# Queueing the scaling of a token tile behind a convolution on VectorE, in the first half of a feed-forward layer

## The chip, the cores and the metric

The kernel runs on one core of one Trainium2 chip. The metric is the device time of one execution in microseconds (us). The core has TensorE (PE in the profile, with its weight loads as PEld), VectorE (DVE), ScalarE (ACT), GpSimd (POOL) and SyncE (SP), which issues nearly all transfers. Each engine works through its own queue in the order that the program was given when it was built.

## The reference, cut to what matters

One layer of a hybrid encoder over 2048 tokens (16 learned ones are put ahead of them) of width 1024. The change lies in its feed-forward half:

```python
f = causal_dwconv(rms_norm(h, norm_ffn_pre[l]) @ ffn_up[l], ffn_conv[l])   # 1024 -> 2 x 2816, 3 taps
gate, val = jnp.split(f, 2, axis=-1)
f = (jax.nn.gelu(gate, approximate=True) * val) @ ffn_down[l]
h = h + rms_norm(f, norm_ffn_post[l])
```

`rms_norm` divides each token by the root of its mean square and multiplies it by a learned gain.

## The kernel before, in words

**Stages.** Input projection, three mixers and the output projection (`w_out_tile`) come first; this last one leaves the hidden state in the scratch array `scr_h`. The up-projection `ffn_up` follows, and then the down-projection. In the profiled run the up-projection runs from 1682 to 2592 us.

**Units.** `ffn_up` works in three super-blocks (`sup`) of 684 tokens each, and in each on 22 column blocks (`j`). One pair (sup, j) is called a unit here, and the units are numbered 0 to 65. A unit has 7 products of 12 matmuls, 84 in all, written to `psu` in three PSUM banks. A Strassen-like scheme makes 7 products do the work of 8, in fp32 split into a high and a low part. PE's queue interleaves the products of neighbouring units. Because products share banks, VectorE and ScalarE act between them: `ga`, `vb` and `u2` are copied out by ScalarE (L1768), and VectorE adds them back (L1784, L1787, L1790). The last product of a unit, p4, goes into a bank that L1787 (written `vb<-psu,vb`) has to have read first. So PE waits there if VectorE is late.

**VectorE in a unit.** Apart from those additions it makes the low parts of the weights (`uw<-uq,uw`, L1603, behind a ScalarE copy, L1602), and two multiply-adds for each of the four convolved blocks (`uy`, L1738, behind ScalarE's L1736). The last of these eight operations reads p4's result, so it stands where p4 of the unit is done. GpSimd multiplies gate by value (L1744), does some of the splits, and makes sums of weights.

**Token tiles.** The tokens of the next super-block are got ready while the current one is computed. The function `between`, called at the head of each unit, fetches the first tile of 128 tokens at j = 1, and at each of j = 2 to 7 fetches one more and calls `ffn_norm` on the one fetched before. A fetch (`ffn_fetch`, L1557, 512 KB from `scr_h` into `xt`) goes through SP's queue. Three buffers hold `xt`. `ffn_norm` scales the tile on VectorE in place (L1564, `xt<-xt,rsv,g_fpre`: by the token's factor `rsv` and by the gain), lets PE transpose it in 8 pieces (L1569, `pst<-ident,xt`), and copies the transposed pieces into `q` (L56 on ScalarE, L58 on VectorE). Super-blocks 1 and 2 have six tiles each. The seven tiles of super-block 0 are scaled during the output projection.

**What sets the order.** A scheduler orders the queues when the program is built: it simulates the engines by its own durations, and hands an engine the next instruction that it takes to be ready. A scaling has no link to the unit in which it is written but the arrival of its tile, so it can be put far ahead of that unit. The context `tc.issue_after(ins)` adds the rule that what is written in it is queued behind `ins` on that engine; it adds no wait at run time.

Of the kernel before, what the change touches and what calls it, by code (L numbers as in the profile page):

```python
# [13 lines left out]
ALU = mybir.AluOpType  # L14
# [155 lines left out]
def mm3(nc, out, ah, al, bh, bl, first, last, more=False):  # L170

    nc.tensor.matmul(out, ah, bh, start=first, stop=False, skip_group_check=more)  # L172
    nc.tensor.matmul(out, ah, bl, start=False, stop=False, skip_group_check=more)  # L173
    nc.tensor.matmul(out, al, bh, start=False, stop=last, skip_group_check=more)  # L174
# [264 lines left out]
class Attn:  # L439
# [43 lines left out]
    def next(self, s):  # L483
        self.turn[s] = (self.turn[s] + 1) % len(self.ring[s])
        return self.ring[s][self.turn[s]]
# [1067 lines left out]
def ffn_fetch(core, pool, scr, s, rows):  # L1553

    xt = pool.tile([P, D], F32, tag="nt_x", name=core.n("xt"))
    t0 = s + META - HALO
    core.nc.sync.dma_start(xt[:rows], scr["h"][t0 : t0 + rows, :])  # L1557
    return xt


def ffn_norm(core, psum, xt, s, rows, rs, gain, quarters, sup):

    nc = core.nc
    nc.vector.scalar_tensor_tensor(xt[:rows], xt[:rows], rs[:rows], gain[:rows], op0=ALU.mult, op1=ALU.mult)  # L1564
    for half in range(2):
        ps = psum.tile([P, 4, P], F32, tag="mm", name=core.n("pst"))
        for k in range(HK):
            k0 = P * (HK * half + k)
            nc.tensor.transpose(ps[:, k, :rows], xt[:rows, k0 : k0 + P], core.ident[:rows, :rows])  # L1569
        for i, blk in enumerate("ab"):  # L1570
            b0 = FBLK * (2 * sup + i)
            a, e = max(s, b0), min(s + rows, b0 + FN)
            if a < e:
                core.evac(quarters[f"{blk}{half}"][:, :, a - b0 : e - b0], ps[:, :, a - s : e - s])
# [5 lines left out]
def ffn_quarters(core, pool, sup):  # L1580

    t = pool.tile([P, len(QUARTERS), HK, FN], F32, tag="q", name=core.n("q"))
    q = {s: t[:, i] for i, s in enumerate(QUARTERS)}
    used = SEQ + HALO - FBLK * (2 * sup + 1)
    if used < FN:
        for s in ("b0", "b1"):
            core.nc.gpsimd.memset(q[s][:, :, used:], 0.0)
    return q
# [129 lines left out]
def ffn_up(core, raws, ring, pool, banks, w_up, cw, scr, between, tokens):  # L1718

    nc = core.nc
    tt, stt = nc.vector.tensor_tensor, nc.vector.scalar_tensor_tensor
    turn = 1
    units = [(sup, j) for sup in range(SUPERS) for j in range(NFF)]
    ahead = UpWeights(core, raws, ring, w_up, scr, 0, 0)
    ws, xs, own = [], [], ahead
    for i in range(UP_FIRST):
        xs.append(tokens(0, i))
        ws.append(ahead.operand(i))  # L1730
    xs.append(tokens(0, UP_FIRST))

    def conv(src, u, j, n):
        y = pool.tile([P, FBLK], F32, tag="uy", name=core.n("uy"), bufs=UY)
        cc = u * NFF + j
        nc.scalar.activation(y[:, :n], src[:, 2 : n + 2], AF.Copy, scale=cw[:, 88 + cc : 89 + cc])  # L1736
        for i in (1, 0):
            stt(y[:, :n], src[:, i : n + i], cw[:, 44 * i + cc : 44 * i + cc + 1], y[:, :n], op0=ALU.mult, op1=ALU.add)  # L1738
        if u == 0:
            nc.scalar.activation(y[:, :n], y[:, :n], AF.Gelu_apprx_tanh)  # L1740
        return y

    def ending(g, v, j, b0, n):
        core.pooled = nc.gpsimd.tensor_tensor(v[:, :n], g[:, :n], v[:, :n], op=ALU.mult)  # L1744
        nc.sync.dma_start(scr["ff"][P * j : P * j + P, b0 : b0 + n], v[:, :n])

    for at, (sup, j) in enumerate(units):
        b0 = [FBLK * (2 * sup + i) for i in range(2)]
        n = [min(FBLK, SEQ - b) for b in b0]
        s = lambda tag: pool.tile([P, FN], F32, tag=tag, name=core.n(tag), bufs=1 if tag == "u2" else 2)[:]  # L1750
        between(sup, j)
        more = at + 1 < len(units)
        if more:
            ahead = UpWeights(core, raws, ring, w_up, scr, *units[at + 1][::-1])
        ws_next, bank = [], {}
        turn ^= 1
        for i, (name, (_, _, at_)) in enumerate(PRODUCTS.items()):
            w, x = ws[i], xs[i]
            first = at_ not in bank
            if first:  # L1760
                bank[at_] = banks[turn].tile([P, 512], F32, tag="up", name=core.n("psu"))[:, :FN]
            ps = bank[at_]
            for k in range(HK):
                mm3(nc, ps, w[:, 0, k], w[:, 1, k], x[:, 0, k], x[:, 1, k], first and k == 0, k == HK - 1, not first)
            behind = nullcontext()
            if name in ("p1", "p5", "p6"):
                t = s({"p1": "ga", "p5": "vb", "p6": "u2"}[name])
                copied = nc.scalar.activation(t, ps, AF.Copy)  # L1768
                ga, vb, u2 = (t, None, None) if name == "p1" else (ga, t, None) if name == "p5" else (ga, vb, t)
                if at == 0:  # L1770
                    behind = core.tc.issue_after(copied.ins)
            with behind:
                if at == 0 and len(ws) < 7:
                    ws.append(own.operand(len(ws)))
                if at == 0 and len(xs) < 7:
                    xs.append(tokens(0, len(xs)))
                if j == NFF - 1 and more:
                    xs[i] = tokens(sup + 1, i)
                if more:
                    ws_next.append(ahead.operand(i))  # L1780
            if name in ("p1", "p5", "p6"):
                pass
            elif name == "p3":
                tt(ps, ps, u2, op=ALU.add)  # L1784
                gb = conv(ps, 0, j, n[1])
            elif name == "p7":
                tt(vb, ps, vb, op=ALU.add)  # L1787
                vb = conv(vb, 1, j, n[1])
            elif name == "p2":
                tt(ps, ps, ga, op=ALU.add)  # L1790
                ga = conv(ps, 0, j, n[0])
                ending(gb, vb, j, b0[1], n[1])
            else:
                va = conv(ps, 1, j, n[0])
                ending(ga, va, j, b0[0], n[0])
        ws = ws_next
# [197 lines left out]
def hybrid_block_kernel(ctx: ExitStack, tc: tile.TileContext, args, out):  # L1994
    a = {s: v[0] if s != "meta_tokens" else v for s, v in args.items()}
    nc = tc.nc
    core = Core(tc, ctx)
# [9 lines left out]
    def pool(es, name, bufs, **kw):  # L2007
        return es.enter_context(tc.tile_pool(name=name, bufs=bufs, **kw))
# [4 lines left out]
    def spread(pl, vec, name):  # L2013
        t = pl.tile([P, D], F32, name=name)
        nc.sync.dma_start(t[:], vec.rearrange("(o n) -> o n", o=1).broadcast_to([P, D]))
        return t

    rsv = base.tile([P, 6 * len(FFN_TILES)], F32, name="rsv")
    cw = base.tile([P, 3 * 2 * NFF], F32, name="ffn_cols")
# [68 lines left out]
    with ExitStack() as p3:  # L2088
        ps_n = pool(p3, "ps_n", 2, space=PSUM, **early)
# [3 lines left out]
        g_fpre = spread(pool(p3, "gf", 1, **early), a["norm_ffn_pre"], "g_fpre")  # L2093
# [6 lines left out]
        rs = {}  # L2100
        with p2:
# [8 lines left out]
            quarters = {0: ffn_quarters(core, qp, 0)}  # L2110
            for i, (f, rows) in enumerate(FFN_TILES):
# [6 lines left out]
                for _ in range(NORMS if i >= LATE else 0):  # L2118
                    if todo:
                        q, f, rows = todo.pop(0)  # L2120
                        xt = ffn_fetch(core, np_, scr, f, rows)
# [15 lines left out]
        def between(sup, j):  # L2137

            for _ in range(1 + (j % 4 == 3) if sup else 0):
                next(later, None)  # L2140
            sup += 1
            if j == 1 and sup < SUPERS:
                quarters[sup] = ffn_quarters(core, qp, sup)
                todo[:] = tiles[sup]
                fetch()
            elif j == 1:
                kept = qp.tile([P, DOWN_KEPT, 2, 512], F32R, tag="q", name=core.n("qd"))
                down.extend(kept[:, i] for i in range(DOWN_KEPT))
            elif sup == SUPERS:
                if j == DOWN_FROM:  # L2150
                    raw = lambda: tmp.tile([P, 512], F32, tag="uq", name=core.n("raw"))[:]
                    ws.append(down_operands(core, raw, lambda: down.pop(0), a["ffn_down"], scr, 0))
            elif fetched:
                q, f, rows, xt = fetched.pop(0)
                fetch()
                ffn_norm(core, ps_n, xt, f, rows, rs[q], g_fpre, quarters[sup], sup)
                if not fetched:
                    sums.append(ffn_sums(core, quarters[sup], lambda: tc.issue_after(core.pooled.ins)))
            else:
                for _ in range(2):  # L2160
                    next(sums[-1], None)
# [79 lines left out]
```

## Time and profile before

| | |
|---|---|
| median of 3 runs (range) | 3065.51 us (3058.34 to 3071.79) |
| the profiled execution's own time | 3063.42 us |
| its span, from the first to the last instruction | 3061.7 us |
| around the span | 1.7 us |
| mean granted clock of PE | 0.971 |
| busy share of PE, DVE, ACT, POOL | 95%, 67%, 48%, 45% |

"Busy" is the time in which an engine had an instruction in work. The ends of matmuls are modelled, so the number of matmuls in a stretch says more about PE's speed than its busy share. In a table of stretches each engine has its busy time and in brackets the number of its instructions. In a timeline, the square brackets give the idle time of the engine just before an instruction and what ended it.

### The profile page before, as it was taken

Reading aid. Unit: us, or ns where it says so; the run is one execution under the profiler, and the core shown is the slowest. Engines: PE = TensorE matmul, PEld = TensorE weight load, DVE = VectorE, ACT = ScalarE, POOL = GpSimd, SP = SyncE. Lnnn points to the kernel's source line nnn. Section 1 sums busy time; section 2 is a strip of 40 time slices with the busy share of each in tenths; the row PEclk is TensorE's granted clock in tenths of the full one; section 3 lists DMA queues with packets and bytes.
Section 4 is the critical chain, followed back from the end, with each engine's and each line's share of the span. In section 5 each row is a group of like instructions: output and inputs, shape, how many; then the busy total and the mean of one; then the engine's idle time right before and its main releaser. Section 6 shows DMA issues by size and latency. Waiting matters only on the chain.

```text
span 3061.7 us, 52809 instructions
## 1 busy us (share of the span) xinstructions
PE 2910.2 (95%) x18694; PEld 2487.6 (81%) x18694; DVE 2057.7 (67%) x3934; ACT 1479.1 (48%) x2853; POOL 1365.7 (45%) x1599
## 2 busy tenths in 40 slices
PE   6998999999989999999999899999999999999998
PEld 6997898888876654566568899999999999787786
DVE  5268645656677785555636888888778777547766
ACT  4245332434346554454534656666566665324333
POOL 1001121122214556566843457445645544556765
PEclk8999999999989898999999999999999999999999
DMA  6776478466654347434336555566677765535454
GB/s 216 244 234 207 163 240 292 154 199 205 211 156 92 88 105 211 109 100 122 75 94 206 171 181 180 172 202 213 209 215 212 220 192 165 171 102 175 148 162 145
DMA packets 467750, 532.58 MB, mean 174 GB/s; under 512 B 85550, under 2 KB 355576, under 8 KB 465932
## 3 DMA queue, kind: packets, MB, share of 16 engines
q1 hardware_dynamic: 466716, 528.27, 56.5%
q8 instruction: 147, 2.41, 0.3%
q14 instruction: 119, 0.97, 0.1%
q0 software_dynamic: 768, 0.93, 0.1%
HBM read 369.11 MB, written 159.95 MB: 173 GB/s over the span
## 4 chain that ended last, share of the span: by engine, by line
PE 34%; DVE 5%; DMA 5%; POOL 3%; issue 3%; ACT 1%; SPq 0%; POOLq 0%; DVEq 0%; ACTq 0%
PE psu L172 8%; PE psu L173 8%; PE psu L174 8%; PE psd L172 2%; PE psd L173 2%; PE psd L174 2%; DMA u<-scr_ff 2%; DMA xt<-scr_h 1%; DVE uw L1603 1%; PE pswo L172 1%; PE pswo L174 1%; PE pswo L173 1%; DVE fo L1603 1%; DVE uy L1738 1%; POOL u L1858 1%
## 5 line engine op out<-in xcount | busy, mean ns | idle before, releaser
L172 PE MATMUL psu<-xo,uw 128*128 128x344 f32 x1848 | 590.8, 323 | 14.7 <-DVE vb L1787 6.9
L173 PE MATMUL psu<-xo,uw 128*128 128x344 f32 x1848 | 593.1, 321 | 0.0
L174 PE MATMUL psu<-xo,uw 128*128 128x344 f32 x1848 | 584.3, 320 | 1.5 <-DVE uw L1603 1.5
L172 PE MATMUL psp<-xh,wh 128*128 128x384 f32 (+2 forms) x1152 | 383.5, 333 | 4.5 <-ACT wh L166 3.0
L174 PE MATMUL psp<-xh,wl 128*128 128x384 f32 (+2 forms) x1152 | 379.5, 330 | 2.6 <-DMA wl<-scr_wk 2.5
L173 PE MATMUL psp<-xl,wh 128*128 128x384 f32 (+2 forms) x1152 | 379.3, 329 | 0.0
L1603 DVE TENSOR_TENSOR uw<-uq,uw 128x512 fp32r<-128x512 f32 x341 | 321.0, 947 | 65.1 <-ACT uw L1602 62.8
L172 PEld LDWEIGHTS psu<-xo,uw 128*128 128x128 f32 x1848 | 347.4, 189 | 19.2 <-DVE vb L1787 9.4
L174 PEld LDWEIGHTS psu<-xo,uw 128*128 128x128 f32 x1848 | 347.2, 189 | 2.4 <-DVE uw L1603 2.3
L173 PEld LDWEIGHTS psu<-xo,uw 128*128 128x128 f32 x1848 | 348.5, 189 | 0.1
L1602 ACT ACTIVATE uw<-uq 128x512 fp32r<-128x512 f32 x462 | 287.5, 627 | 107.5 <-PE psu L174 46.6
L686 ACT ACTIVATE p<-sc,bias 128x512 f32<-128x512 f32 (+4 forms) x352 | 197.0, 589 | 194.9 <-PE sc L682 162.1
L559 DVE TENSOR_REDUCE mc<-mx 128x1 f32<-128x512 f32 (+6 forms) x352 | 190.2, 564 | 114.1 <-PE mx L554 87.2
L1738 DVE SCALAR_TENSOR_TENSOR uy<-psu,ffn_cols,uy 128x342 f32<-128x342 f32 (+1 forms) x396 | 223.7, 567 | 62.3 <-ACT uy L1736 60.9
L1744 POOL TENSOR_TENSOR uy<-uy,uy 128x342 f32<-128x342 f32 (+1 forms) x132 | 140.0, 1061 | 252.7 <-DVE uy L1738 70.1
L725 POOL TENSOR_TENSOR acc<-acc,p 128x512 f32<-128x512 f32 (+3 forms) x208 | 221.7, 1068 | 53.1 <-DVE acc L725 23.9
L1603 POOL TENSOR_TENSOR uw<-uq,uw 128x512 fp32r<-128x512 f32 x121 | 177.6, 1468 | 148.0 <-ACT uw L1602 129.5
L172 PEld LDWEIGHTS psp<-xh,wh 128*128 128x128 f32 x1152 | 221.7, 192 | 11.6 <-issue 4.2
L174 PEld LDWEIGHTS psp<-xh,wl 128*128 128x128 f32 x1152 | 220.8, 192 | 12.0 <-issue 5.7
L173 PEld LDWEIGHTS psp<-xl,wh 128*128 128x128 f32 x1152 | 221.3, 192 | 7.5 <-issue 5.4
L1603 DVE TENSOR_TENSOR fo<-u,fo 128x896 fp32r<-128x896 f32 x88 | 109.0, 1240 | 118.8 <-ACT fo L1602 118.8
L1602 ACT ACTIVATE fo<-u 128x896 fp32r<-128x896 f32 x88 | 81.1, 922 | 200.9 <-POOL u L1859 103.8
(470 smaller groups left out, 6470.3 us busy)
## 6 DMA issues: line engine op xcount, KB each, us to landing
uq<-scr_us SPq DMA_DIRECT2D x220, 256.0 KB
uq<-in_ffn_up_dram SPq DMA_DIRECT2D x209, 256.0 KB
wl<-scr_wk SPq DMA_DIRECT2D x48, 512.0 KB
wh<-scr_wk SPq DMA_DIRECT2D x48, 512.0 KB
u<-scr_ff SPq DMA_DIRECT2D x88, 256.0 KB
scr_ff<-uy SPq DMA_DIRECT2D x110, 171.0 KB
raw<-in_w_in_dram SPq DMA_DIRECT2D x24, 512.0 KB
scr_wk<-wh SPq DMA_DIRECT2D x24, 512.0 KB
```

Source lines behind the costliest of these rows:

```text
L172: nc.tensor.matmul(out, ah, bh, start=first, stop=False, skip_group_check=more)
L173: nc.tensor.matmul(out, ah, bl, start=False, stop=False, skip_group_check=more)
L174: nc.tensor.matmul(out, al, bh, start=False, stop=last, skip_group_check=more)
L559: self.reduced = nc.vector.tensor_reduce(mc[:rows, i, ci : ci + 1], ps[:rows, : e - a], axis=AX.X, op=ALU.max)
L686: last = nc.scalar.activation(p[:rows, :w], ps[:rows, :w], AF.Exp, bias=bias[:rows, j : j + 1])
L725: eng.tensor_tensor(a, ps_[0][0][:rows, c0:n] if start and i == 1 else a, p[:rows, : n - c0], op=ALU.add)
L1602: core.nc.scalar.activation(hi, src, AF.Copy)
L1603: (eng or core.nc.vector).tensor_tensor(lo, src, hi, op=ALU.subtract)
L1738: stt(y[:, :n], src[:, i : n + i], cw[:, 44 * i + cc : 44 * i + cc + 1], y[:, :n], op0=ALU.mult, op1=ALU.add)
L1744: core.pooled = nc.gpsimd.tensor_tensor(v[:, :n], g[:, :n], v[:, :n], op=ALU.mult)
L1858: tt(s3, a0, b0, op=ALU.subtract)
```

## The change

The scaling inside `ffn_norm` is put into a context given by the caller. The caller in `between` gives one that queues the scaling behind the last convolution operation traced so far, which is that of the unit ahead (unit j-1 for the tile of unit j). The calls during the output projection are left as they were. `conv` keeps the instruction in `core.conved`. No operation is added or taken away.

```diff
-def ffn_norm(core, psum, xt, s, rows, rs, gain, quarters, sup):
+def ffn_norm(core, psum, xt, s, rows, rs, gain, quarters, sup, after=nullcontext):
     nc = core.nc
-    nc.vector.scalar_tensor_tensor(xt[:rows], xt[:rows], rs[:rows], gain[:rows], op0=ALU.mult, op1=ALU.mult)
+    with after():
+        nc.vector.scalar_tensor_tensor(xt[:rows], xt[:rows], rs[:rows], gain[:rows], op0=ALU.mult, op1=ALU.mult)
...
         for i in (1, 0):
-            stt(y[:, :n], src[:, i : n + i], cw[:, 44 * i + cc : 44 * i + cc + 1], y[:, :n], op0=ALU.mult, op1=ALU.add)
+            core.conved = stt(
+                y[:, :n], src[:, i : n + i], cw[:, 44 * i + cc : 44 * i + cc + 1], y[:, :n], op0=ALU.mult, op1=ALU.add
+            )
...
-                ffn_norm(core, ps_n, xt, f, rows, rs[q], g_fpre, quarters[sup], sup)
+                behind = lambda: tc.issue_after(core.conved.ins)
+                ffn_norm(core, ps_n, xt, f, rows, rs[q], g_fpre, quarters[sup], sup, behind)
```

All line numbers of the changed kernel are higher by 1 in `ffn_norm` and by 3 behind `conv`. The scheduler makes a new order of all queues from it. Three places show how.

VectorE before, around the scaling of the fifth tile of super-block 1 (`xt_18889`, which belongs to unit 6). `uy_18542<-psu_18395` is the last convolution of unit 2; `psu_18589`, `ga_18584` and the like belong to unit 3.

```order
L1603 TENSOR_TENSOR uw_18627<-uq_18624,uw_18627 128x512
L1564 SCALAR_TENSOR_TENSOR xt_18889<-xt_18889,rsv,g_fpre 128x1024
L1738 SCALAR_TENSOR_TENSOR uy_18542<-psu_18395,ffn_cols,uy_18542 128x342
L1603 TENSOR_TENSOR uw_18645<-uq_18642,uw_18645 128x512
L1738 SCALAR_TENSOR_TENSOR uy_18542<-psu_18395,ffn_cols,uy_18542 128x342
L1603 TENSOR_TENSOR uw_18668<-uq_18565,uw_18668 128x512
L1603 TENSOR_TENSOR uw_18689<-uq_18569,uw_18689 128x512
L1790 TENSOR_TENSOR psu_18676<-psu_18676,ga_18584 128x344
L1784 TENSOR_TENSOR psu_18589<-psu_18589,u_3257_18622 128x344
```

VectorE now, around the same tile. `uy_19058<-psu_18914` is the last convolution of unit 5; `psu_19099`, `vb_19112` and the like belong to unit 6.

```order
L1604 TENSOR_TENSOR uw_19175<-uq_19173,uw_19175 128x512
L1739 SCALAR_TENSOR_TENSOR uy_19058<-psu_18914,ffn_cols,uy_19058 128x342
L1565 SCALAR_TENSOR_TENSOR xt_18889<-xt_18889,rsv,g_fpre 128x1024
L1604 TENSOR_TENSOR uw_19198<-uq_19196,uw_19198 128x512
L1787 TENSOR_TENSOR psu_19099<-psu_19099,u_3335_19131 128x344
L1793 TENSOR_TENSOR psu_19183<-psu_19183,ga_19092 128x344
L1604 TENSOR_TENSOR uw_19268<-uq_19245,uw_19268 128x512
L1739 SCALAR_TENSOR_TENSOR uy_19156<-psu_19099,ffn_cols,uy_19156 128x342 x2
L58 COPY q_18219<-pst_19073 128x4x128
L1790 TENSOR_TENSOR vb_19112<-psu_19079,vb_19112 128x344
```

The scaling stood ahead of the last convolution of unit 2, four units before its own; it stands behind that of unit 5 now. All twelve go the same way. In super-block 1 each of the six is now queued at the head of its own unit, 2 to 7. Before, its first three were queued during the output projection, the fourth in unit 0 and the fifth and sixth in units 3 and 4, and the first three tiles of super-block 2 in units 5, 6 and 7, sixteen units and more ahead of theirs. All six of super-block 2 are now queued in units 24 to 29.

PE before, at the transposes of the first tile of super-block 1 (`xt_18220`): in unit 0, between its second and third product.

```order
L173 MATMUL psu_18069<-xo_18019,uw_18025 128x344
L174 MATMUL psu_18069<-xo_18019,uw_18025 128x344
L1569 MATMUL pst_18383<-ident,xt_18220 128x128 x4
L1569 MATMUL pst_18389<-ident,xt_18220 128x128 x4
L172 MATMUL psu_18040<-xo_18028,uw_18034 128x344
```

PE now, at the same transposes: three matmuls short of the end of the sixth product of unit 2.

```order
L173 MATMUL psu_18395<-xo_18061,uw_18327 128x344
L174 MATMUL psu_18395<-xo_18061,uw_18327 128x344
L1570 MATMUL pst_18383<-ident,xt_18220 128x128 x4
L1570 MATMUL pst_18389<-ident,xt_18220 128x128 x4
L172 MATMUL psu_18395<-xo_18061,uw_18327 128x344
```

The transposes of a tile now stand late in the tile's own unit, most of a unit behind its scaling. Units 2 to 7 carry one tile each, where units 0 and 2 to 6 carried one each before.

SP before, at the fetch of the fourth tile of super-block 1 (`xt_18721`): directly behind the last stores of the output projection.

```order
L1506 DMA scr_h<-wx_17833 128x1024
L1506 DMA scr_h<-wx_17908 128x1024
L1557 DMA xt_18721<-scr_h 128x1024
L1678 DMA uq_18208<-in_ffn_up_dram 128x4x128
L1678 DMA uq_18222<-in_ffn_up_dram 128x4x128
```

SP now, at the same fetch: at the end of unit 2, since it takes the buffer that the first tile frees.

```order
L1679 DMA uq_18790<-scr_us 128x512
L1679 DMA uq_18807<-scr_us 128x512
L1557 DMA xt_18721<-scr_h 128x1024
L1679 DMA uq_18830<-scr_us 128x512
L1748 DMA scr_ff<-uy_18495 128x342
```

The fetches of the fifth and later tiles move back by about one unit as well, while the scalings move back by more, so that each fetch now has two units and more until its scaling.

## The prediction

> **What bounds the kernel now.** I read the page first.
>
> ```profile
> PE 2910.2 (95%) x18694; PEld 2487.6 (81%) x18694; DVE 2057.7 (67%) x3934; ACT 1479.1 (48%) x2853; POOL 1365.7 (45%) x1599
> ```
>
> PE is in work for 95% of the span, so the change can only pay where PE stands still in the up-projection. The next view, busy time by stretch, is cut at every 84th matmul on `psu`: one unit per row for units 0, 1, 4, 5, 6 and 7, then units 0 to 7 together, 2 to 7 together, 8 to 20, and 22 to 29.
>
> ```profile
> 1682.01:1700.47 18.46, 15.16 (x94) 14.04 (x92) 14.03 (x19) 15.55 (x29) 1.74 (x1) 1.00 0.36 117
> 1700.47:1715.97 15.50, 13.78 (x87) 13.16 (x85) 15.50 (x20) 7.78 (x15) 10.91 (x7) 1.00 0.56 183
> 1744.66:1765.93 21.27, 16.90 (x93) 16.60 (x93) 19.51 (x28) 9.82 (x21) 14.59 (x10) 0.84 0.56 175
> 1765.93:1780.10 14.17, 14.17 (x95) 14.14 (x94) 11.47 (x19) 7.90 (x16) 3.98 (x3) 1.00 0.58 175
> 1780.10:1796.79 16.69, 14.68 (x94) 14.13 (x93) 14.36 (x20) 9.62 (x20) 11.19 (x9) 1.00 0.58 189
> 1796.79:1812.10 15.31, 13.53 (x87) 13.24 (x86) 11.70 (x19) 6.70 (x14) 4.31 (x4) 1.00 0.57 177
> 1682.01:1812.10 130.09, 116.90 (x722) 113.60 (x721) 108.03 (x153) 74.21 (x148) 63.15 (x43) 0.97 0.55 172
> 1715.97:1812.10 96.13, 87.96 (x545) 86.40 (x546) 78.49 (x116) 50.88 (x106) 50.49 (x36) 0.96 0.59 182
> 1812.10:1984.62 172.52, 172.52 (x1095) 172.52 (x1094) 144.54 (x219) 106.94 (x213) 110.35 (x86) 1.00 0.58 178
> 1997.87:2111.64 113.77, 112.64 (x722) 111.23 (x721) 97.81 (x148) 69.09 (x141) 56.37 (x44) 1.00 0.69 210
> ```
>
> The columns are length, then PE, PEld, DVE, ACT, POOL, PE's granted clock, DMA share and GB/s. Units 8 to 20 take 172.52 / 13 = 13.27 us each without a gap. Unit 5 takes 14.17 with the 8 transposes of a tile in it, so a tile costs PE 0.90. These are the floors. Unit 4 is 7.1 us over its floor, unit 6 2.5, unit 7 (no tile) 2.0. Now the scalings in this stretch, and what PE waited for.
>
> ```profile
> 1742.75 1.28 DVE L1564 SCALAR_TENSOR_TENSOR xt<-xt,rsv,g_fpre 128x1024 f32<-128x1024 f32 x1 [6.17 <-DMA xt<-scr_h]
> ...
> 1787.74 1.44 DVE L1564 SCALAR_TENSOR_TENSOR xt<-xt,rsv,g_fpre 128x1024 f32<-128x1024 f32 x1 [1.68 <-DMA xt<-scr_h]
> ...
> 1803.91 1.28 DVE L1564 SCALAR_TENSOR_TENSOR xt<-xt,rsv,g_fpre 128x1024 f32<-128x1024 f32 x1 [3.57 <-DMA xt<-scr_h]
> ```
>
> ```profile
> DVE xt L1564 <- DMA xt<-scr_h: 15.8, 5, 6.2
> DVE uy L1738 <- ACT uy L1736: 1.7, 3, 0.7
> ```
>
> ```profile
> 1749.59 0.50 DVE L1787 TENSOR_TENSOR vb<-psu,vb 128x344 f32<-128x344 f32 x1
> 1750.14 0.66 PE L172 MATMUL psu<-xo,uw 128*128 128x344 f32 x1 [4.37 <-DVE vb L1787]
> 1750.60 0.49 PE L173 MATMUL psu<-xo,uw 128*128 128x344 f32 x1
> ...
> 1755.47 0.41 PE L172 MATMUL psu<-xo,uw 128*128 128x344 f32 x1
> ...
> 1790.58 0.43 PE L172 MATMUL psu<-xo,uw 128*128 128x344 f32 x1 [1.36 <-ACT vb L1768]
> ...
> 1807.12 0.42 PE L172 MATMUL psu<-xo,uw 128*128 128x344 f32 x1 [1.78 <-ACT vb L1768]
> ```
>
> The middle fence is VectorE's waits in units 2 to 7 (us, times, longest): in 96.13 us it worked for 78.49 and stood for 15.8 at five scalings whose tile was still on its way. All that is queued behind a scaling stands with it: the last convolution, the splits, the three additions. In unit 4 the addition L1787 came so late that PE stood 4.37 us; in units 6 and 7 ScalarE, itself held up by a late convolution, copied `vb` late. The transfer is simply asked for too late:
>
> ```profile
> 1735.55 0.37 SPq L1557 DMA_DIRECT2D xt<-scr_h  x1
> ```
>
> 1735.55 to 1742.75 is 7.2 us, and VectorE reached the scaling 1.0 us after the request.
>
> **The change part by part.** No operation comes or goes; a scaling, its transposes, copies and fetch move.
>
> *The waits at the tile, units 2 to 7.* Each fetch now has two units, over 26 us, until its scaling, against 7.2 us to land; the cover is 19 us. So the 15.8 us of standing go. What is late next is VectorE's own work. It did 78.49 us with five scalings; with the sixth and 0.68 for a copy it has 80.5, and PE's floor for six units with a tile is 6 x 14.17 = 85.0.
>
> ```profile
> L1564 DVE SCALAR_TENSOR_TENSOR xt<-xt,rsv,g_fpre x18: 1273/1284/2166, 1601.0 to 2063.7; 128x1024 f32<-128x1024 f32 x18
> 1731.86 0.68 DVE L58 COPY q<-pst 128x512 f32<-128x512 f32 x1
> ```
>
> To this come VectorE's waits for ScalarE. They were 1.7 us here, while it ran late; in units 8 to 20 VectorE is short of work for 172.52 - 144.54 = 28.0 us, 2.2 a unit, or 12.9 in six. VectorE's stretch is then 82.2 to 93.4, and PE's between 85.0 and 93.4. I take 86.0, near the lower end, because a VectorE that runs late finds ScalarE done, as these very units show. This gives 96.13 - 86.0 = **10.1 us** (2.7 to 11.1). The slow matmuls behind the 4.37 us gap are in it: 17 matmuls from 1750.60 to 1755.47 took 4.87 us where the quiet units need 17 x 0.158 = 2.7, so 2.2 of unit 4's 7.1 are clock, and the row's granted clock is 0.84. [...]
>
> *Where the scaling lands.* Ahead of it now stands the last convolution, which follows p4; behind it stand a split and the additions L1784 and L1790, which wait for PE's second and third product behind p4 anyway, at 12 x 0.158 = 1.9 us a product. One scaling of 1.28 fits there. Its longest took 2.17; at that price six would cost 5.3 us more, which the range holds. [...]
>
> *Units 0 and 1.* The fourth tile's scaling, its fetch and the first tile's transposes and copies leave.
>
> ```profile
> 1685.78 1.04 PE L1569 MATMUL pst<-ident,xt 128*128 128x128 f32 x8
> 1689.21 0.42 PE L172 MATMUL psu<-xo,uw 128*128 128x344 f32 x1 [2.39 <-ACT ga L1768]
> 1691.27 1.28 DVE L1564 SCALAR_TENSOR_TENSOR xt<-xt,rsv,g_fpre 128x1024 f32<-128x1024 f32 x1 [0.82 <-DMA xt<-scr_h]
> ...
> 1693.21 0.42 PE L174 MATMUL psu<-xo,uw 128*128 128x344 f32 x1 [0.79 <-DVE uw L1603]
> 1715.97 0.39 PE L172 MATMUL psu<-xo,uw 128*128 128x344 f32 x1 [0.99 <-DVE uy L1738]
> ```
>
> The transposes stood in front of a wait for ScalarE's `ga`, so taking them away only lengthens that wait: nothing gained in unit 0, and the 0.90 that they cost elsewhere is in the six floors above. The split that PE waited 0.79 for is queued behind the scaling and its 0.82 of waiting, so that wait goes: 0.8 (0 to 1.0). In unit 1 VectorE was busy for 15.50 of 15.50 us, and PE waited 0.99 for a convolution at its end; 1.28 and a copy taken from ahead of it remove that: 1.0 (0 to 1.0).
>
> *Output projection.* Three scalings leave it. PE had no gap there, so nothing changes (0):
>
> ```profile
> 1640.00:1660.00 20.00, 20.00 (x89) 1.00 0.51 160
> ```
>
> *Super-block 2's tiles, units 22 to 29.* The floor is 8 x 13.27 + 6 x 0.90 = 111.6, the row above 113.77. VectorE's waits there were
>
> ```profile
> DVE xt L1564 <- DMA xt<-scr_h: 4.7, 2, 3.1
> ```
>
> and they go, while three scalings (3.9 us) come. I take 1.0 gained (2.2 gained to 3.0 lost).
>
> *Sum.* 10.1 + 0.8 + 1.0 + 1.0 = 12.9 us off the profiled execution's 3063.42 (its span 3061.7 and 1.7 around it): **3050.5 us**. That execution is 2.1 under the median of the runs, 3065.51, against which the forecast is 15.0 us or 0.49% down. The later stages are PE's own and are moved as a whole.
>
> **The rivals.** *VectorE becomes the bound.* With no tile to wait for, its queue holds PE up by about one scaling a unit: 12 x 1.28 = 15.4 us of new waits against 12.9 gained, 3066. For it: VectorE had no slack at all in unit 1, and its work and its usual waits add up to 93.4. Against: 80.5 of work stand against 85.0. Chance 0.12.
>
> *The stall only changes its name.* PE is held by weights instead, whose transfers had time to run ahead while PE stood: gain 0 to 4, 3061. For it: the DMA share is 0.56 to 0.69 here. Against: in units 8 to 20 the same share, 0.58, feeds PE without a gap. Chance 0.10.
>
> *Slower.* VectorE's lateness is not worked off within a unit but piles up until L1787 is over 4 us late, as at 1750.14, and PE's clock falls each time. One such stall costs unit 4's 7.1 us; one in every second unit of the twelve makes 6 x 7.1 = 42.6, less 12.9, so 3093. It sets in from VectorE's work and waits reaching 14.17 a unit; the upper bound above, 93.4 / 6 = 15.6, is over that, the work alone, 13.4, is not. Chance 0.08.
>
> That the scheduler ignores the rule is excluded: the order shows all twelve behind their convolutions.
>
> **How the numbers follow.** The forecast's case, gain 8 to 17, has 0.70. About 0.5% of the time, 15.3 us or 3050.2, is what a measurement can tell from no change. The forecast lies at this bound if the median before is the measure, and 2.4 us short of it if the profiled execution is; part of its case therefore counts as faster, 0.42, and the rest, 0.28, as the same, with the first two rivals: 0.50. Slower is 0.08. The range takes in the first two rivals above, and below the full floors (11.1 + 1.0 + 1.0 + 2.2 = 15.3) with the 7 us that the lowest run lay under the median: 3040 to 3068.
>
> **What would show it right or wrong.** (Lines by the numbers of before.) Right: no wait of L1564 for `xt<-scr_h` in units 2 to 7 and 22 to 29; unit 4 near 14.2 us; units 2 to 7 at 86; no granted clock of 0.84 there; the wait of 0.99 gone from the end of unit 1. Wrong: PE waits for `vb`, L1787, or for `uw`, in each of units 2 to 7; units 22 to 29 over 115 us; or a stretch behind unit 30 that changes by over 3 us, which no step here accounts for.

## The result: 9.5 us faster, and not where all of it was forecast

The changed kernel takes 3053.33 us (median of 12 runs, 3047.27 to 3058.81); the kernel before, timed beside it, 3062.87 (12 runs, 3054.65 to 3071.79). The ratio is 0.9969 with an interval of 0.996 to 0.9977: 0.31% faster, which the interval tells from no change, but short of the 0.5% from which the prediction counts a change as faster. The forecast was 3050.5. One run of the kernel before, timed beside e12 below, took 5538 us, far beyond all others, and is left out of the medians there.

The profiled execution took 3049.84 us with a span of 3048.1, 13.6 us less than the profiled one of before. The table cuts both by stage; the units are cut at every 84th matmul on `psu`, as in the prediction.

| stage | before | after | difference | forecast |
|---|---|---|---|---|
| all ahead of unit 0 | 1682.01 | 1674.35 | -7.66 | 0 |
| unit 0 | 18.46 | 19.41 | +0.95 | -0.8 |
| unit 1 | 15.50 | 13.37 | -2.13 | -1.0 |
| units 2 to 7 | 96.13 | 85.02 | -11.11 | -10.1 |
| units 8 to 21 | 185.77 | 185.82 | +0.05 | 0 |
| units 22 to 29 | 113.77 | 111.66 | -2.11 | -1.0 |
| units 30 to 65 | 480.69 | 479.99 | -0.70 | 0 |
| down-projection, to the end of the span | 469.4 | 478.5 | +9.1 | 0 |

The rows of after, busy time by stretch: unit 0, unit 1, units 4, 6 and 7, units 2 to 7 together, 8 to 20, 22 to 29, 30 to 65, and the down-projection.

```profile
1674.35:1693.76 19.41, 16.14 (x85) 15.85 (x84) 15.81 (x22) 15.67 (x29) 2.87 (x2) 0.82 0.31 96
1693.76:1707.13 13.37, 13.37 (x87) 13.27 (x86) 13.37 (x17) 8.31 (x16) 11.25 (x9) 1.00 0.63 209
1735.51:1749.67 14.16, 14.16 (x94) 14.14 (x93) 12.87 (x20) 9.00 (x18) 10.14 (x8) 1.00 0.53 167
1763.83:1777.99 14.16, 14.16 (x95) 14.14 (x94) 13.46 (x16) 8.10 (x17) 10.59 (x7) 1.00 0.47 153
1777.99:1792.15 14.16, 14.16 (x94) 14.12 (x94) 13.31 (x21) 8.03 (x17) 6.80 (x5) 1.00 0.74 223
1707.13:1792.15 85.02, 85.02 (x555) 84.77 (x554) 80.22 (x116) 50.70 (x104) 52.45 (x34) 1.00 0.67 205
1792.15:1964.70 172.55, 172.55 (x1093) 172.55 (x1093) 142.66 (x220) 106.96 (x213) 110.48 (x86) 1.00 0.60 182
1977.97:2089.63 111.66, 111.66 (x721) 111.30 (x721) 102.00 (x149) 68.23 (x139) 58.08 (x44) 1.00 0.73 215
2089.63:2569.62 479.99, 478.28 (x3027) 477.71 (x3025) 369.51 (x588) 299.95 (x589) 242.81 (x204) 1.00 0.69 203
2569.62:3048.10 478.48, 445.67 (x1874) 354.45 (x1872) 304.49 (x368) 166.56 (x278) 287.49 (x359) 0.97 0.45 149
```

In units 2 to 7 PE is in work for 85.02 of 85.02 us, at a granted clock of 1.00: the floor itself. The last two stages of before, for comparison:

```profile
2111.64:2592.33 480.69, 478.84 (x3027) 477.79 (x3025) 368.84 (x588) 298.75 (x589) 244.23 (x204) 1.00 0.68 203
2592.33:3061.70 469.37, 442.57 (x1874) 354.04 (x1872) 304.05 (x367) 166.58 (x278) 291.49 (x360) 0.97 0.46 152
```

The twelve scalings of after, by their line (shortest, median and longest in ns), then all that PE waited for in the whole up-projection, then VectorE's waits in units 2 to 7 (us, times, longest):

```profile
L1565 DVE SCALAR_TENSOR_TENSOR xt<-xt,rsv,g_fpre x12: 1268/1276/1897, 1716.0 to 2081.3; 128x1024 f32<-128x1024 f32 x12
```

```profile
PE psu L172 <- ACT ga L1771: 3.3, 1, 3.3
PE psu L172 <- DVE vb L1790: 1.7, 2, 1.1
```

```profile
DVE uw L1604 <- ACT uw L1603: 2.0, 4, 0.7
DVE uy L1739 <- ACT uy L1737: 1.5, 2, 1.2
DVE xo L1604 <- ACT xo L1603: 0.8, 1, 0.8
```

No scaling waits for `xt<-scr_h` any more. This is VectorE's timeline in unit 4, where the 4.37 us gap was. The scaling stands behind the last convolution, and the additions L1787, L1793 and L1790 follow in time:

```profile
1742.85 0.56 DVE L1739 SCALAR_TENSOR_TENSOR uy<-psu,ffn_cols,uy 128x342 f32<-128x342 f32 x1
1743.33 1.46 DVE L1565 SCALAR_TENSOR_TENSOR xt<-xt,rsv,g_fpre 128x1024 f32<-128x1024 f32 x1
1744.72 1.78 DVE L1604 TENSOR_TENSOR uw<-uq,uw 128x512 fp32r<-128x512 f32 x1
1746.42 0.51 DVE L1787 TENSOR_TENSOR psu<-psu,u 128x344 f32<-128x344 f32 x1
1746.85 0.51 DVE L1793 TENSOR_TENSOR psu<-psu,ga 128x344 f32<-128x344 f32 x1
...
1749.81 0.51 DVE L1790 TENSOR_TENSOR vb<-psu,vb 128x344 f32<-128x344 f32 x1
```

### The profile page after: what moved, and what is told of

The parts are those of the page before. It is cut to its first block, busy times and chain, and to the rows that moved or that the text cites. A ratio compares the mean times of both kernels' runs of the same rounds, so it can differ in the third digit from the quotient of the medians.

```text
span 3048.1 us, 52845 instructions
## 1 busy us (share of the span) xinstructions
PE 2903.8 (95%) x18694; PEld 2482.9 (81%) x18694; DVE 2057.4 (67%) x3934; ACT 1482.4 (49%) x2853; POOL 1364.0 (45%) x1599
## 4 chain that ended last, share of the span: by engine, by line
PE 38%; DVE 3%; DMA 3%; POOL 3%; issue 2%; ACT 1%; POOLq 0%; DVEq 0%; SPq 0%; ACTq 0%
PE psu L172 9%; PE psu L173 9%; PE psu L174 9%; PE psd L174 2%; PE psd L173 2%; PE psd L172 2%; DMA u<-scr_ff 2%; PE pswo L172 1%; PE pswo L174 1%; PE pswo L173 1%; DVE fo L1604 1%; POOL u L1861 1%; PE pst L1570 1%; POOL u L1859 0%; POOL u L1860 0%
## 5 line engine op out<-in xcount | busy, mean ns | idle before, releaser
L1747 POOL TENSOR_TENSOR uy<-uy,uy 128x342 f32<-128x342 f32 (+1 forms) x132 | 147.3, 1116 | 243.1 <-DVE uy L1739 62.7
```

## The experiments

All twelve in one table, stage lengths from each run's profile in us, the ratio to the kernel before from the timed runs. "PE +" is how many more instructions PE has than in the kernel before, its waits that take an instruction of their own included; the last group of experiments is about it.

| kernel | units 2 to 7 | up-projection | down-projection | PE + | ratio (interval) |
|---|---|---|---|---|---|
| before | 96.13 | 910.3 | 469.4 | 0 | |
| e1, before again | 96.10 | 910.5 | 472.5 | 0 | |
| after | 85.02 | 895.3 | 478.5 | 16 | 0.9969 (0.996 to 0.9977) |
| e2, after again | 85.28 | 895.8 | 478.3 | 16 | 0.9959 (0.9945 to 0.9974) |
| e3, rule in super-block 1 only | 88.22 | 902.1 | 478.4 | 9 | 0.9981 (0.9966 to 0.9996) |
| e4, rule in super-block 2 only | 91.18 | 902.3 | 472.4 | 8 | 0.9975 (0.9964 to 0.9986) |
| e5, late fetch | 98.22 | 917.0 | 477.7 | 11 | 1.004 (1.0026 to 1.0054) |
| e6, one buffer | 88.59 | 899.2 | 475.6 | 19 | 0.9985 (0.9972 to 0.9999) |
| e7, scaled twice | 94.71 | 909.9 | 477.5 | 11 | 1.0013 (0.9999 to 1.0027) |
| e8, scaled four times | 100.26 | 923.1 | 476.2 | 15 | 1.0064 (1.0043 to 1.0086) |
| e9, after, down later | 85.05 | 895.7 | 478.9 | 16 | 0.9962 (0.9946 to 0.9977) |
| e10, before, down later | 100.69 | 915.0 | 472.0 | 0 | 1.0012 (0.9997 to 1.0027) |
| e11, spare work | 87.46 | 896.9 | 478.0 | 18 | 0.9972 (0.9958 to 0.9986) |
| e12, before, 16 more | 99.04 | 911.3 | 477.3 | 16 | 1.0006 (0.9991 to 1.0021) |

### What repeats: e1 and e2

The kernel before and the changed kernel again, without an edit.

> The kernel before, unchanged, for a second profile of it. In the first pair of profiles the up-projection (units 0 to 65) went from 910.4 to 895.3 us, 15.0 less, while the median of twelve runs each fell by 9.5. If the stalls are set by the order alone, units 0 to 7 take 130 again and units 22 to 29 114, and the missing 5.5 us are in another stage, made slower by the change. If the stalls vary from one execution to the next, units 0 to 7 take some 121 to 127 this time, and the up-projection as a whole about 905.

> The changed kernel, unchanged, for a second profile of it and for more runs. Units 0 to 7 at 118, units 22 to 29 at 111.7, each within 1 us, since nothing waits for a tile any more. Ratio to before 0.995 to 0.998. If the down-projection was slowed by the change, it takes 478 us from the last product of unit 65 to the end again, 9 more than before; if that was the execution, 469 to 478.

The up-projection came out as 910.54 and 895.81, within 0.6 us of the first profiles: the gain of 14.7 to 15.0 there belongs to the kernel. All that lies ahead of unit 0 took 1674 to 1692 us in the fourteen profiles, with no relation to the edit (1682.0 and 1684.1 for before, 1674.4 and 1678.5 for after, 1690.0 for e9): the 7.66 of the table above is the execution's own and no gain. The down-projection does differ between the two kernels: 469.4 and 472.5 against 478.5 and 478.3. Of the 15 us, some 6 to 9 were given back there.

### The two halves of the rule: e3 and e4

```diff
-ffn_norm(core, ps_n, xt, f, rows, rs[q], g_fpre, quarters[sup], sup, behind)
+ffn_norm(..., sup, behind if sup == 1 else nullcontext)   # e3; sup == 2 in e4
```

> The rule for the six tiles of super-block 1 alone. The order then has the first three tiles of super-block 2 scaled in units 6, 7 and 8, each shortly behind its fetch. If the wait for the transfer is the cost: units 1 to 5 at their floors, waits of 1.5 to 6 us for a tile left in units 6 to 8 and PE standing 1 to 4 us there, units 22 to 29 at 113 to 114; 3 to 6 us slower than the whole change. If it is the place among the convolutions that counts: units 2 to 7 at 85 as in the whole change.

> The rule for the six tiles of super-block 2 alone. Super-block 1's tiles keep their old places, so the waits in units 0, 3 and 4 stay, and those of units 5 to 7 go with their three scalings. If the wait for the transfer is the cost: unit 4 again 4 to 7 us over its floor, units 5 to 7 at their floors, units 22 to 29 at 111.7; 4 to 7 us faster than before. The two parts together then come to about the whole; if they share a cause that is not the wait, either part alone gives nearly all.

Each half alone takes 8 us off the up-projection (8.2 and 8.0; both together 15.0), so they add up but for 1.2. Units 2 to 7 need both. With the rule for super-block 1 alone they took 88.2: one tile of super-block 2 was still scaled there ahead of its arrival (VectorE stood 1.3 us), and PE stood 1.9 us for an addition and 0.8 for a tile. With that for super-block 2 alone they took 91.2. So sending the three scalings away that came from sixteen units later gives 5.0 of the 11.1 us in these units; the rest of e4's gain lies mostly in units 22 to 29 (111.5 us). The down-projection is long with the first half alone and short with the second.

### Is it the transfer? e5 and e6

e5 keeps the rule and takes its lead away: the fetch is queued on SP behind the last store of the unit ahead, so that tile and scaling come due together again. e6 keeps the order of PE and VectorE and gives the twelve tiles one buffer in place of three.

```diff
-                fetch()
+                with tc.issue_after(core.stored.ins):   # e5, in the same call as ffn_norm
+                    fetch()
...
-    xt = pool.tile([P, D], F32, tag="nt_x", name=core.n("xt"))
+    xt = pool.tile([P, D], F32, tag=tag, name=core.n("xt"), bufs=bufs)   # e6: "nt_x", 2 and "nt_y", 1
```

> The rule is kept, but each of the twelve fetches is queued on SP behind the last store of the unit ahead, so that it loses its lead of two units. The scheduler, which takes a tile to land sooner than it does, puts the scaling about ten VectorE instructions behind the convolution. If the wait for the transfer is the cost: VectorE waits for a tile at most of the twelve again, 1 to 5 us each, and the up-projection loses 5 to 25 us of the 15.0 that it gained (900 to 920 us). If standing behind the convolution is what helps: 895 to 898, as with the whole change.

> The rule is kept, and the twelve tiles share one buffer of their own (the output projection has the other two). The order of PE and VectorE in units 1 to 65 is that of the whole change; a fetch now has to wait for the transposes of the tile before, and has some 10 us until its scaling instead of two units. If the lead matters only as far as it covers the landing (7.2 us before): waits for a tile of at most 1 to 3 us in a few units, up-projection 895 to 900 us. If more lead is what helps, waits in all twelve and 905 or more.

In e5 the wait for the tile is back, and longer than in the kernel before. VectorE's first line of waits and PE's, up to about unit 30:

```profile
DVE xt L1565 <- DMA xt<-scr_h: 36.4, 12, 6.1
```

```profile
PE pst L1570 <- DVE xt L1565: 17.6, 9, 5.5
```

All twelve scalings wait, and the gain is gone, with a loss of 6.6 us on top (916.96 against 910.32). But e5 changed two things: the lead is gone, and the order came out with the transposes close behind the scaling, so that PE itself stood for them. e6 changes the lead alone. There three of the twelve scalings wait, PE stands 2.3 us for two of the tiles, and 3.9 of the 15 us go:

```profile
DVE xt L1565 <- DMA xt<-scr_h: 4.9, 3, 2.4
```

So in e5 the rule without the lead was worth nothing, and e6 shows that the lead itself counts; what pays is that the fetch leads the scaling.

### Is VectorE the limit? e7, e8 and e11

e7 and e8 do each of the twelve scalings two and four times over; e11 adds a sum over the scaled tile that nothing reads.

```diff
-    with after():
-        nc.vector.scalar_tensor_tensor(xt[:rows], xt[:rows], rs[:rows], gain[:rows], ...)
+    for _ in range(1 if after is nullcontext else 2):   # e7; 4 in e8
+        with after():
+            nc.vector.scalar_tensor_tensor(xt[:rows], xt[:rows], rs[:rows], gain[:rows], ...)
...
+    with after():   # e11, behind the single scaling
+        nc.vector.tensor_reduce(spare[:rows], xt[:rows], axis=AX.X, op=ALU.add)
```

> Each of the twelve scalings is done twice (the values are then wrong; time alone counts): VectorE gets 1.28 us more in each of units 2 to 7 and 24 to 29. If VectorE has 2 us and more to spare in these units, as the changed kernel's trace has it: units 2 to 7 at 85 to 87, and the up-projection within 3 us of 895. If VectorE is at its limit there: 12 x 1.28 = 15 us more, 910.

> Each of the twelve scalings is done four times (values wrong, time alone counts): 3.84 us more VectorE work in each of twelve units. VectorE's work in units 2 to 7 is then about 80.5 + 6 x 3.84 = 103.5 us against PE's 85.0, so there VectorE must become the bound: units 2 to 7 at 103 to 110. In units 24 to 29 the work is lower by 1.5 us a unit: some 90 to 98 us for the six. Up-projection 915 to 935 us. If VectorE's order does not matter to PE at all, 895.

> The changed kernel with one more VectorE operation per tile behind each of the twelve scalings: a sum over the scaled tile, 128x1024, written to a column that nothing reads. VectorE gets about as much more work as with the doubled scaling, but the transposes do not wait for it and stand within 0.1 unit of where the changed kernel has them (the doubled scaling moved them by up to 0.2 of a unit, to just behind it, and the up-projection took 909.9 in place of 895.3). Theory V, VectorE's time was the limit there: up-projection 905 to 915, PE waits on psu for VectorE's additions. Theory T, the place of the transposes was: 895 to 898, no wait of PE for a scaled tile.

e7 missed: 94.7 in units 2 to 7, and the up-projection lost 14.7 of its 15.0 us. The scalings took 1.66 us each on average, so VectorE's work in units 2 to 7 came to 91.30 us, over PE's 85.0:

```profile
1724.78:1819.49 94.71, 87.09 (x546) 85.19 (x545) 91.30 (x120) 49.14 (x103) 54.18 (x34) 0.98 0.61 186
```

PE's waits up to about unit 30 show where this was felt:

```profile
PE pst L1571 <- DVE xt L1566: 9.8, 7, 3.4
...
PE psu L172 <- DVE vb L1791: 1.0, 2, 0.5
```

PE waited 9.8 us for the scaled tile itself, and 1.0 for an addition. The new order had put the transposes just behind the second scaling. So two causes are mixed in e7, VectorE's work and the place of the transposes. e11 leaves the transposes nearly where the changed kernel has them and adds less work. Its two operations on VectorE in units 2 to 7 and the stretch, then PE's first two waits up to about unit 30:

```profile
L1565 DVE SCALAR_TENSOR_TENSOR xt<-xt,rsv,g_fpre 128x1024 f32<-128x1024 f32 x6 | 8.4, 1397 | 0.0
L1568 DVE TENSOR_REDUCE spare<-xt 128x1 f32<-128x1024 f32 x6 | 7.2, 1204 | 0.0
```

```profile
1711.58:1799.04 87.46, 85.60 (x555) 84.73 (x554) 84.78 (x124) 51.04 (x108) 52.07 (x34) 1.00 0.64 198
```

```profile
PE psu L172 <- ACT ga L1774: 3.2, 1, 3.2
PE pst L1573 <- DVE xt L1565: 1.8, 1, 1.8
```

1.2 us more per tile on VectorE, 14.4 in all, cost the up-projection 1.6 us, and no PE wait for an addition is among the first lines. Units 2 to 7 alone took 2.4 us more, 1.8 of them in the one wait for a scaled tile; units 22 to 29, at 111.5, nothing more. So VectorE, busy for 80.2 of 85.0 us in the changed kernel, is not the limit there, and what it stands idle shrinks as its work grows (4.8 us there, 2.7 in e11). But the room in units 2 to 7 is small: e11's 84.78 us of work just stay under PE's 85.0, e7's 91.30 do not. How much of e7's loss comes from that work and how much from the place of the transposes is not separated by these runs. At four scalings VectorE is the bound beyond doubt: in units 2 to 7 of e8 it was in work for 99.30 of 100.26 us.

```profile
1719.70:1819.96 100.26, 88.48 (x546) 85.89 (x545) 99.30 (x126) 50.51 (x105) 51.95 (x32) 0.98 0.56 168
```

### The down-projection: e9, e10 and e12

No operation of this stage is touched, but the order at the passage from `psu` to `psd` comes out a little differently. One constant, the column block from which the weights of the down-projection are prepared, moves that order, and it was used to cross the two: e9 was to be the changed kernel with the passage as in before, e10 the kernel before with the passage as in the changed ones.

```diff
-DOWN_FROM = 14
+DOWN_FROM = 15
```

> The changed kernel with one constant moved: the weights of the down-projection are prepared from column block 15 of the last super-block on, not from 14. All twelve scalings and transposes stand as in the changed kernel; but the order at the passage from the up-projection to the down-projection comes out as in the kernel before (PE's last 4915 rows are the same as there; the changed kernel's only from 1731 rows before the end). Open is why the down-projection took 469 to 473 us in the three profiles that have before's order there and 475 to 479 in all others. Theory A, the order at that passage costs it: last matmul on psu to the end 469 to 473, up-projection 895 to 896, ratio to the kernel before 0.992 to 0.995. Theory B, the rule itself costs it (an up-projection without stalls leaves something later in another state): 475 to 479, ratio 0.995 to 0.997, as in the repeat of the changed kernel.

> The other corner: the kernel before, without the rule, with the same constant at 15. Its order at the passage to the down-projection comes out like that of the changed kernels (same as the kernel before only in PE's last 1731 rows). Theory A: last matmul on psu to the end 475 to 479 though no scaling is queued behind anything, up-projection 909 to 911, ratio 1.001 to 1.003. Theory B: 469 to 473, ratio 0.9995 to 1.0005.

Theory A (the order at the passage costs the time) fell with e10: 472.0, though by the records PE's queue in this stage is that of the changed kernel but for the places of two matmuls. e9, at 478.9, says less than was hoped: by the records its PE queue is not that of before in the first 30 us of the stage, but a third order. What was left is a count: the kernels with 469 to 473 us have 0 or 8 more instructions on PE than the kernel before, those with 475 to 479 have 9 to 19. The length does not grow with the count, though (478.4 with 9, 475.6 with 19). e12 adds instructions to the kernel before.

```diff
-        for k in range(HK):
+        for k in 2 * list(range(HK)) if (sup, s) == (0, 0) else range(HK):
             k0 = P * (HK * half + k)
             nc.tensor.transpose(ps[:, k, :rows], xt[:rows, k0 : k0 + P], core.ident[:rows, :rows])
```

> The kernel before, without the rule, with the eight transposes of the two-token tile of super-block 0 done twice (the second time over the same result): eight more matmuls of 2x2 and eight more weight loads, 16 more instructions on PE during the output projection, and nothing else. Why this: the order at the passage to the down-projection has been excluded as what costs the down-projection its 6 us. What still separates the profiles at 469 to 473 us from those at 475 to 479 is the number of PE's instructions: the records have 18914, 18914, 18914 and 18922 weight loads and semaphore instructions in the short ones, 18923 to 18933 in the long ones (a rule that moves instructions also changes how many of PE's waits need an instruction of their own). In the long ones one of the 16 pieces of a fetch of u lands 1.2 to 2.3 us behind the other 15 in nearly every one of the last pairs, and one transfer of 16 KB of PE's instructions starts in just that stretch; PE then stands 1.0 to 1.6 us. This kernel has 18930 by count, as the changed kernel. Theory P, the place of PE's instruction loads decides: last matmul on psu to the end 475 to 479 with the up-projection still at 909 to 915, PE's gaps of 1.0 to 1.6 us once per pair, ratio to the kernel before 1.001 to 1.003. Theory Q, something else that comes with the rule decides (the number of GpSimd's instructions, which stays as in the kernel before here, or the queues' state): 469 to 473, ratio 0.9995 to 1.001.

The 18930 in this expectation is not right: by the records e12 has 8 more weight loads, which makes 18922 in that count, and 8 more matmuls, 18702. Together these are 16 more instructions, as many as in the changed kernel. The count is not all that changed against the kernel before, since the order came out anew as well, in the up-projection and at the passage. But from the start of the down-projection on, the records of e12 show the same order, by operation and tile, as those of e10 on all five engines. Against e10, with 472.0 us, the 16 instructions are what is left in this stage, and e12's down-projection took 477.3 us, without the rule and with an up-projection of 911.3. PE's waits in 180 us of that stage in before, after, e9, e10 and e12, in this order:

```profile
PE psd L172 <- ACT fo L1602: 2.7, 6, 0.5
```

```profile
PE psd L172 <- ACT fo L1603: 6.1, 12, 1.2
```

```profile
PE psd L172 <- ACT fo L1603: 7.0, 11, 0.9
```

```profile
PE psd L172 <- ACT fo L1602: 2.8, 7, 0.5
```

```profile
PE psd L172 <- ACT fo L1602: 6.7, 11, 0.9
```

`fo` comes from `u`, which GpSimd sums once its fetch has landed. GpSimd's wait at the same fetch in before, e10, after and e12:

```profile
2982.12 0.46 POOL L1856 TENSOR_TENSOR u<-u 128x128 f32<-128x128 f32 x1 [5.88 <-DMA u<-scr_ff]
```

```profile
2987.75 0.46 POOL L1856 TENSOR_TENSOR u<-u 128x128 f32<-128x128 f32 x1 [5.64 <-DMA u<-scr_ff]
```

```profile
2968.20 0.46 POOL L1859 TENSOR_TENSOR u<-u 128x128 f32<-128x128 f32 x1 [6.79 <-DMA u<-scr_ff]
```

```profile
2985.30 0.88 POOL L1856 TENSOR_TENSOR u<-u 128x128 f32<-128x128 f32 x1 [7.28 <-DMA u<-scr_ff]
```

In the transfer records of after and e12, 15 of the 16 pieces of this fetch have landed when the last one is still 1.2 and 1.7 us away; in before and e10 it follows within 0.11. About every 30 us a single packet of 16 KB runs on q8, a DMA queue of the kind "instruction" (147 packets in before and in after, 15 of them in this stage), and takes 0.9 to 2.3 us. Between two of them lie 234 to 282 of PE's records in this stage of before and 226 to 288 in that of after, 256 in the median of either whole execution, so it is taken for the load of PE's own instructions. In after and e12 it begins 0.6 us ahead of the landing of this fetch's first piece, in before and e10 0.7 and 0.5 us behind it.

All fourteen profiles point the same way. Of the 84 fetches of `u` in each, the last piece lands more than 0.8 us behind the other 15 in 2, 2 and 1 of them in before, e1 and e10, in 6 in e4, and in 7 to 16 in the ten kernels with a long down-projection. Of these 110 late pieces, 108 land 1.9 to 4.2 us after the start of an instruction load. So the late pieces go with the loads, and there are more of them where the stage is long; that the load pushes the piece back is inferred from times.

That 16 instructions more bring this about and cost the stage 5 to 8 us rests on one profile, e12's. It was also taken on another chip than e10's, and the kernel before was timed but not profiled on that chip. The medians don't settle it: e12's 3073.64 against 3071.34 leaves 2.3 us, of which the up-projection has 1.0, with an interval of 4.6 to either side. Taking the up-projection's difference off the difference of the medians in the same way leaves 0.9 to 7.6 us, 3.9 on average, for the nine other kernels with a long down-projection, and 1.0 and -2.4 for e4 and e10. So the loss is there in the timed runs of the group, smaller than in the profiles, and those of e12 can't tell it from nothing. A version of the changed kernel with PE's count moved back wasn't run.

## Why the prediction was right, and where it was right by accident

The time was right (3050.5 against 3053.33), and so was "the same" as the likeliest class. That the total came so close is in part luck. The forecast gain of 12.9 us was one of the up-projection, which gained 15.0; the down-projection, set at nothing, gave 9.1 back in the profiled execution; and 7.7 ahead of unit 0 that no edit explains came on top. The 13.6 between the two profiles is the sum of these three. The medians differ by 9.5, 3.4 less than forecast.

- **Units 2 to 7** (10.1 forecast, 2.7 to 11.1 the bounds): 11.1, the upper bound. The mechanism is shown: no scaling waits, unit 4 takes 14.16, no granted clock under 1.00, and e6, which shortens the lead and nothing else, brings waits back with a part of the loss. The size was off by the 1.0 that was left for VectorE's waits. The "VectorE's stretch 82.2 to 93.4" that set the range added its usual waits to its work as if they stayed; they were 4.3 us (2.0 + 1.5 + 0.8), and 80.2 of work with them just fit.
- **"One scaling of 1.28 fits there"**: it does, even the longest, 1.90. The median scaling is 1.28, as before. There is little more room: e11's 1.2 us a tile cost 2.4 in units 2 to 7.
- **Unit 0** (0.8 forecast, 0 to 1.0): missed. The wait for `uw` went, and the wait for `ga` grew from 2.39 to 3.3 by the transposes' 0.9, both as the prediction had it. What it left out is the clock: 0.82 granted in after's unit 0, where before had 1.00, so that the unit took 0.95 longer. In e2, with the same wait, unit 0 took 18.31 at 0.91, so the term came out at about 0.15 there, and the rest is how long the clock stays down (at 0.5 for 3.41 us in e2, 6.83 in after).
- **Unit 1** (1.0): 2.1 in after, 1.1 in e2. Units 0 and 1 together are 1.2 shorter in both (32.78 and 32.75 against 33.96); 1.8 was forecast. What after lost in unit 0 it made good in unit 1, where e2 still waits 0.9 for `u` and after does not.
- **Units 22 to 29** (1.0, 2.2 gained to 3.0 lost): 2.1, again at the floor.
- **"The later stages are PE's own and are moved as a whole"**: this is the step that failed, by the prediction's own sign, a stretch behind unit 30 that changes by over 3 us. The down-projection is not PE's own: even in before PE stands 2.7 us in 180 for `fo`, behind fetches that GpSimd waits for, and in after 6.1. The stage took 478.5 and 478.3 us with the change against 469.4 and 472.5, so 6 to 9 us of the gain were given back. That 16 instructions more on PE do this is the best account so far, by e12 and the late pieces, and not settled. Without this loss the up-projection's full 15 us would be left, close to 0.5%.
- **The rivals.** VectorE as the bound did not occur with the change (its 80.2 us of work left PE without a wait in units 2 to 7), but it is near: e7's 91.30 are over the floor, and in e8 VectorE is the bound. The stall that only changes its name did not occur either: PE waited for no weights in the up-projection. The pile-up did not occur.

## What to carry to other kernels

Where an in-order engine waits for a transfer, queue the waiting operation behind work that is surely due earlier, and see that the transfer is asked for well ahead of it: the order without the lead (e5, with 917.0 us in the up-projection against 910.3) is worse than nothing. Check each stage that an edit "can't touch" against two profiles of each kernel before a gain is summed: here the stretch ahead of unit 0 differed by up to 18 us between executions with no relation to the edit, and the down-projection, which no edit touched, by 6 to 9. An experiment that adds work to test a limit also changes the order; compare the work with the floor, and look at who waits (`pst`, not `vb`), before calling it the limit.

## What the hardware showed that was not expected

**Instruction loads.** See e12: in its one profile, eight transposes more (the same eight take PE 0.65 us in before) at 1597 us, with their weight loads, go with 5 to 8 us more in a stage that begins nearly 1000 us later.

**The clock in steps.** Unit 0 of e1 and of before have the same wait of 2.39 us for `ga`, e2 and after the same 3.3. The rows of unit 0 in e1 and e2:

```profile
1684.06:1702.53 18.47, 16.07 (x94) 15.63 (x92) 14.05 (x19) 15.56 (x29) 1.74 (x1) 0.91 0.37 116
```

```profile
1678.46:1696.77 18.31, 15.04 (x85) 14.75 (x84) 14.71 (x20) 15.40 (x29) 1.88 (x2) 0.91 0.32 102
```

Granted clocks of 1.00 and 0.91 for the same wait in the one pair, 0.91 and 0.82 in the other. The clock records of the traces have it at 0.5 for 3.41 us in e2 and for 6.83 in after, one step or two, and the rows agree: 0.09 x 18.31 x 2 = 3.3 us and 0.18 x 19.41 x 2 = 7.0. In before and after together there are 54 records at 0.5; all but the last of each execution are of 3.41 us or of two to five times that. A wait of 2.39 us was enough for a step in e1; what decides between none, one and two is not shown. In all nine kernels with the wait of 3.2 to 3.3 us the clock fell in unit 0 (0.91 in eight, 0.82 in after); in the five with 2.4 it fell in e1 and e12 and stayed at 1.00 in before, e4 and e10. The second step made after's unit 0 1.1 us longer than e2's.

**Without the rule, an edit elsewhere moves these units.** Units 2 to 7 took 96.1 us twice in the kernel before, and 100.7 and 99.0 in e10 and e12, whose edits lie elsewhere; with the full rule and nothing else added there they took 85.0, 85.3 and, in e9 with the edit of e10, 85.1.
